# Second macaron step of a hybrid trunk layer: ten of 22 hidden tiles by seven block products

## The chip, the cores and the metric

The kernel runs on one core of a Trainium2 chip. The core has a matrix engine (TensorE, PE in the profile; its weight loads are shown apart as PEld), VectorE (DVE), ScalarE (ACT), GpSimd (POOL) and SyncE (SP), which issues the transfers. Each engine works through its own queue in order and waits on semaphores that the others raise. The metric is device time in microseconds, of the whole program, median of several runs.

## What is computed

One layer of a decoder trunk over 512 tokens of 1024 features, all in float32: a macaron half-step with a gated feed-forward, a mixer (attention and a state-space branch), a second macaron half-step, a gated embedding, a last norm. The change is in the second half-step, which is this, with `x` of 512 x 1024, `w1` and `w3` of 1024 x 2816 and `w2` of 2816 x 1024:

```python
def rmsnorm(x, g):
    y = xf * lax.rsqrt(jnp.mean(xf * xf, axis=-1, keepdims=True) + EPS)
    return (y * g.astype(jnp.float32)).astype(x.dtype)

def swiglu(x, w1, w3, w2):
    return (jax.nn.silu(x @ w1) * (x @ w3)) @ w2

h = h + 0.5 * swiglu(rmsnorm(h, g_ffn2[i]), w1_b[i], w3_b[i], w2_b[i])
```

`x @ w1` is called the gate product here, `x @ w3` the linear product. The 2816 hidden features are 22 tiles of 128.

## The kernel before

Activations lie transposed, features on the 128 partitions and the 512 tokens along the row, so the residual stream is eight tiles `X[k]` of 128x512. Matmuls take 128x128 of a weight as the stationary operand and 128x512 of the activation as the moving one. For accuracy each float32 operand is split into a rounded high part and the remainder, and each product is three matmuls (`mm3`, lines 234 to 237): high x high, low x high, high x low. The split of a weight half (128x512, four 128x128 blocks, loaded whole from HBM into `wraw`, five buffers) is a cast on ACT for the high part (`split_w`, L159) and a subtraction on DVE for the low part (helper `tt`, L74).

The work is a list of units, each with its weight sources, its steps of matmuls and the operations that follow a step. `run` goes through the units step by step and writes the instructions out in that order; nothing reorders them later. At the start of a step it casts the weights that the next unit will need (`convert`), then issues the evictions that have come due, then chains, then deferred work and the subtractions of the new weights, then the step's matmuls. An eviction listed as `(step, d, fn)` is issued `d` steps after the next step begins. So on ACT and DVE the place in the queue is set by these numbers alone.

A half-step (`ffn_units`) works in three parts of 7, 7 and 8 hidden tiles. For every hidden tile there is a unit for the gate product and one for the linear product, each two steps of 12 matmuls; then come eight output tiles of the down projection over the tiles of the part, `X[m] += 0.5 * ...`. The evictions of a tile: `gate_a` multiplies the gate product by the norm's row `nrm.r` on DVE and takes the tanh on ACT, `gate_b` forms silu up to a factor on DVE, `lin_a` scales the linear product on DVE, `lin_b` multiplies the two on DVE and casts the high part of the hidden tile on ACT (L369), `lin_c` subtracts for the low part on DVE. `lin_a` has d = 0 and `lin_b` has d = 1 (0 for the last tile of a part).

After this half-step comes the gate of the embedding (`gate_units`). Twelve of its sixteen weight halves are split ahead of time, two per unit, in units counted from the end of the half-step's list: `U2[j // 2 - 20]`. They go into four buffers of tag `m2` and into the shared pool `g4` of 27 buffers, where the normed inputs and the hidden tiles lie too.

Of the kernel before, what the change touches and what calls it, by code (L numbers as in the profile page):

```python
# [15 lines left out]
L = 512  # L16
# [5 lines left out]
EPS = 1e-6  # L22
FIRST = [(0, 2), (2, 4), (4, 8)]
PREP = 5
FEW = 3
SCORES = [(n, n + 1, n + 2) for n in (0, 4, 8, 12)]
VALUES = [7, 11, 15, 18]
# [14 lines left out]
def hybrid_trunk_kernel(ctx: ExitStack, tc: tile.TileContext, xT, pT, w13a, w2a, w13b, w2b, wqk, wv, ws, wf,  # L42
# [71 lines left out]
    selr = const.tile([128, 8], F32R, name="selr")  # L114


    qsel = [const.tile([128, L], F32R, name=f"qsel{j}") for j in range(2)]
    kcum = [const.tile([128, L], F32R, name=f"kcum{j}") for j in range(2)]
    HALF = [slice(0, 64), slice(64, 128)]


# [65 lines left out]
    def convert(u, nxt, h):  # L187

        last = h == len(u.steps) - 1
        res = []  # L190
        if nxt is not None:
            res = [(nxt, i) for i in range(len(nxt.srcs)) if nxt.parts[i] is None and (i == h or last)]
        return res + [(v, i) for hh, v, i in u.extra if hh == h]

    def order_weights(units):
# [8 lines left out]
    def run(units):  # L204
        while dma_at[0] < RAWS:
            wdma()
        for ui, u in enumerate(units):
            nxt = units[ui + 1] if ui + 1 < len(units) else None
            for f in u.starts:
                f()  # L210
            for h, step in enumerate(u.steps):
                rest = [split_w(v, i) for v, i in convert(u, nxt, h)] if u.ahead else []
                run_posts(evicts)
                advance(chains)
                while late:
# [23 lines left out]
    def gemm_steps(box, key, rhs, n, half=None):  # L239


        h = min(4, n)

        def part(k0, k1):
            def f(u):
                if k0 == 0:
                    box[key] = bank()
                for k in range(k0, k1):
                    mm3(box[key], *u.w(k if half is None else half * 4 + k % 4), *rhs(k), k == 0, k == n - 1)
            return f  # L250
        return [part(0, h), part(h, n)]
# [90 lines left out]

    PARTS = [range(0, 7), range(7, 14), range(14, 22)]

    def ffn_units(nrm, w13, w2, final, skip_first=False):
        units = []
        ready = lambda: nrm.r is not None
        for pi, part in enumerate(PARTS):
            hid = {}
            for f in part:  # L350
                box = {}

                def gate_a(box=box):
                    box["t"] = tmp(base="t1")
                    tt(box["t"], box[0], nrm.r, MUL)
                    box["h"] = tmp(base="th")
                    act(box["h"], box["t"], AF.Tanh, scale=0.5)

                def gate_b(box=box):
# [12 lines left out]
                def lin_c(box=box, hid=hid, f=f):  # L372
                    tt(hid[f][:, 1, :], box["t"], raw32(hid[f][:, 0, :]), SUB)

                if f == 0 and skip_first:
                    units.append((box, [(1, 0, gate_a), (1, 1, gate_b), (1, 1, lin_a), (1, 2, lin_b),
                                        (1, 3, lin_c)], ready))
                    continue
                e = 0 if f == part[-1] else 1
                after = [[(0, gate_a), (1, gate_b)], [(0, lin_a), (e, lin_b), (e + 1, lin_c)]]  # L380
                if f == 0:

                    steps = [[gemm_steps(box, wi, nrm.pair, KD, wi)[h] for wi in range(2)] for h in range(2)]
# [1224 lines left out]
```

## Time and profile before

| | us |
|---|---|
| median of three runs | 1006.03 (1005.78 to 1007.55) |
| profiled execution, device time | 1005.87 |
| its span, first to last instruction | 1004.1 |
| PE busy | 992.2 |
| DVE busy | 642.5 |
| ACT busy | 419.1 |
| POOL busy | 85.5 |

The second macaron step runs from about 594 to 950 us of the span. Matmuls are pipelined and the ends of their records are modelled, so a matmul's cost is read from the distance between the starts of neighbours, not from its duration. DVE and ACT records overlap a little for the same reason: what an operation costs its queue is the distance to the next start.

### The profile page before, as it was taken

To read this page: it belongs to the slowest core of one execution; us is meant where nothing else is said; L and a number is where in the kernel's file an instruction comes from. 1 tells how busy PE (TensorE), PEld (TensorE's weight loads), DVE (VectorE), ACT (ScalarE), POOL (GpSimd) and SP (SyncE) were. 2 spreads that over 40 slices of the span, in tenths; PEclk is the share of its full clock that TensorE was granted. 3 is DMA by queue.
4 is the path that set the end of the run, shared out by engine and by line. 5 is a ranking of instruction groups with operands and counts; after the bars stand their busy time and mean duration, and the time that the engine had idled before them with its cause. 6 is when DMAs were issued, how large, how long until landed. Compare 5 with 4: busy or idle time off the path is not lost.

```text
span 1004.1 us, 13382 instructions
## 1 busy us (share of the span) xinstructions
PE 992.2 (99%) x4800; PEld 826.5 (82%) x4800; DVE 642.5 (64%) x1252; ACT 419.1 (42%) x793; POOL 85.5 (9%) x87
## 2 busy tenths in 40 slices
PE   9999999999999999999999999999999999999996
PEld 7888888888878889887888888888888888888876
DVE  6668788767755555889987865443454436646443
ACT  6333233332244444469995443322333224434232
POOL 0440000001000001004651010000000000000000
PEclk9999999999999999999999999999999999999999
DMA  6432332323245332222212233333323334533101
GB/s 210 146 96 83 110 103 92 88 84 108 95 109 129 94 95 74 64 64 73 79 60 74 87 114 95 102 92 100 100 89 97 93 105 148 168 103 95 43 35 49
DMA packets 56915, 96.57 MB, mean 96 GB/s; under 512 B 10176, under 2 KB 14912, under 8 KB 56848
## 3 DMA queue, kind: packets, MB, share of 16 engines
q1 hardware_dynamic: 56432, 94.62, 30.8%
q0 software_dynamic: 416, 1.08, 0.3%
q8 instruction: 38, 0.62, 0.3%
q14 instruction: 29, 0.24, 0.1%
HBM read 92.41 MB, written 2.10 MB: 94 GB/s over the span
## 4 chain that ended last, share of the span: by engine, by line
PE 86%; issue 9%; ACT 2%; DVE 1%; POOL 1%; DMA 1%; SPq 0%; POOLq 0%; DVEq 0%; ACTq 0%
PE ps L235 27%; PE ps L237 27%; PE ps L236 27%; PE ps L1487 1%; PE ps L1098 1%; POOL lg L1090 1%; DMA x<-xT 1%; PE ps L315 0%; PE ps L329 0%; PE ps L1144 0%; PE ps L1143 0%; PE ps L647 0%; ACT gt L80 0%; ACT xhl L80 0%; SPq L1458 0%
## 5 line engine op out<-in xcount | busy, mean ns | idle before, releaser
L235 PE MATMUL ps<-xhl,whi 128*128 128x512 f32 x816 | 320.3, 393 | 0.0
L237 PE MATMUL ps<-xhl,whi 128*128 128x512 f32 x816 | 317.8, 389 | 0.0
L236 PE MATMUL ps<-xhl,wlo 128*128 128x512 f32 x816 | 317.7, 389 | 0.0
L159 ACT CAST whi<-wraw 128x512 fp32r<-128x512 f32 x324 | 195.9, 607 | 239.9 <-PE ps L237 177.0
L74 DVE TENSOR_TENSOR wlo<-wraw,whi 128x512 fp32r<-128x512 f32 x324 | 216.7, 674 | 5.8 <-ACT whi L159 5.6
L237 PEld LDWEIGHTS ps<-xhl,whi 128*128 128x128 f32 x816 | 153.2, 188 | 32.3
L235 PEld LDWEIGHTS ps<-xhl,whi 128*128 128x128 f32 x816 | 153.2, 188 | 31.9 <-issue 1.0
L236 PEld LDWEIGHTS ps<-xhl,wlo 128*128 128x128 f32 x816 | 153.3, 188 | 31.2
L235 PE MATMUL ps<-h,whi 128*128 128x512 f32 x352 | 137.3, 390 | 0.0
L237 PE MATMUL ps<-h,whi 128*128 128x512 f32 x352 | 137.0, 389 | 0.0
L236 PE MATMUL ps<-h,wlo 128*128 128x512 f32 x352 | 137.0, 389 | 0.0
L77 DVE SCALAR_TENSOR_TENSOR x<-ps,x 128x512 f32<-128x512 f32 x48 | 33.2, 691 | 95.2 <-PE ps L237 95.1
L77 DVE SCALAR_TENSOR_TENSOR t<-ps,rbc 128x512 f32<-128x512 f32 x44 | 30.3, 690 | 76.3 <-PE ps L237 76.3
L236 PEld LDWEIGHTS ps<-h,wlo 128*128 128x128 f32 x352 | 66.1, 188 | 13.7
L237 PEld LDWEIGHTS ps<-h,whi 128*128 128x128 f32 x352 | 66.1, 188 | 13.7
L235 PEld LDWEIGHTS ps<-h,whi 128*128 128x128 f32 x352 | 66.1, 188 | 13.7
L74 DVE TENSOR_TENSOR t<-ps,rbc 128x512 f32<-128x512 f32 x44 | 30.4, 691 | 71.1 <-PE ps L237 65.0
L80 ACT ACTIVATE th<-t 128x512 f32<-128x512 f32 x44 | 27.8, 632 | 91.1 <-DVE t L74 91.1
L369 ACT CAST h<-t 128x512 fp32r<-128x512 f32 x44 | 27.4, 622 | 81.3 <-DVE t L74 81.3
L319 POOL TENSOR_TENSOR rc<-ms,mhalf 128x4 f32<-128x4 f32 x6 | 8.1, 1344 | 519.2 <-DVE ms L318 519.2
L1090 POOL TENSOR_SCALAR lg<-lg,rs 128x128 f32<-128x128 f32 (+3 forms) x32 | 37.8, 1196 | 97.9 <-issue 78.7
L80 ACT ACTIVATE xhl<-x,colt 128x512 fp32r<-128x512 f32 x32 | 23.0, 725 | 47.9 <-DVE x L77 41.0
(254 smaller groups left out, 1104.0 us busy)
## 6 DMA issues: line engine op xcount, KB each, us to landing
wraw<-w13b SPq DMA_DIRECT2D x88, 256.0 KB, 2.9
wraw<-w13a SPq DMA_DIRECT2D x84, 256.0 KB, 2.8
wraw<-w2a SPq DMA_DIRECT2D x32, 256.0 KB, 2.7
wraw<-w2b SPq DMA_DIRECT2D x32, 256.0 KB, 2.7
wraw<-wqk SPq DMA_DIRECT2D x16, 256.0 KB, 2.8
wraw<-wout SPq DMA_DIRECT2D x16, 256.0 KB, 2.7
wraw<-wgate SPq DMA_DIRECT2D x16, 256.0 KB, 2.8
wraw<-w2a SPq DMA_DIRECT2D x16, 192.0 KB, 2.4
```

The lines of the kernel that those rows point to most:

```text
L74: V.tensor_tensor(out, a, b, op)
L77: V.scalar_tensor_tensor(out, a, s, b, op0, op1)
L80: S.activation(out, in_, f, **kw)
L159: S.copy(hi[:, 0:n], w[:, 0:n])
L235: T.matmul(ps, lh, rh, start=start, stop=False)
L236: T.matmul(ps, ll, rh, start=False, stop=False)
L237: T.matmul(ps, lh, rl, start=False, stop=stop)
L319: G.tensor_tensor(rc[:, 0:n], ms[:, 0:n], mhalf[:, 0:n], ALU.pow)
L369: S.copy(hl[:, 0, :], box["t"])
L1090: G.tensor_scalar(x, x, rs[h2][:, j:j + 1], None, MUL)
L1098: T.transpose(ps[:, j * 128:(j + 1) * 128], lg[h2][:, j * 128:(j + 1) * 128], ident)
L1487: T.matmul(box0[wi], fw[wi][2 if i == 1 else 1][:, k], n1.pair(k)[i == 2], start=k + i == 0, stop=k + i == KD + 1)
```

## The change

Twelve tiles stay as they were ("plain"), ten become "quick", by the string `PLAIN`: tiles 3, 5, 7, 9, 11, 13, 14, 16, 18 and 20. A quick tile takes its gate and linear products together as a product of 2x2 blocks: the weights in four blocks (gate and linear, first and second half of the 1024 features), the input in four (first and second half of the features, lower and upper 256 tokens). In place of eight block products it forms seven, from sums of blocks (Winograd's form of Strassen's scheme). Each of the seven is a step of 4 slices x 3 passes, 12 matmuls with 256 columns. They collect in two PSUM banks: several products add onto the same area, and between them ACT copies the area out (`p1`, `p5`, `u2`, `u3`).

The sums of weights are formed on POOL from four whole blocks, which are loaded into four spare tiles (`qsel` and `kcum` of the attention, now in a pool) with two more for results (`maskp` and a buffer of `rbc`). Each of the seven weight operands is split as before, cast on ACT and subtraction on DVE, into the four `m2` buffers, three steps ahead of its product (`AHEAD`). The differences of the input are formed once, during the first tiles (`halves`): scaled copies on ACT, differences on POOL, split on ACT and DVE, eight more tiles of `g4`. `beside` puts the sums and splits at steps of the units around the quick tile, by the nominal step lengths in `lasts`. Because `g4` is fuller now, the early splits of the gate weights move to the last eight units of the half-step (`U2[j // 2 - 8]`).

The core of the diff:

```diff
+PLAIN = 'PPPQPQPQPQPQPQQPQPQPQP'
...
-    qsel = [const.tile([128, L], F32R, name=f"qsel{j}") for j in range(2)]
-    kcum = [const.tile([128, L], F32R, name=f"kcum{j}") for j in range(2)]
+    qsel = [spare_tile(F32R, "qsel") for _ in range(2)]
+    kcum = [spare_tile(F32R, "kcum") for _ in range(2)]
...
+            self.hooks, self.lasts = {}, [2.72] * len(steps)
...
+                rest += [f for f in [f() for f in u.hooks.get(h, [])] if f]
                 run_posts(posts)
...
+    def halves(nrm, goff):
...
+        for k in range(4):
+            xa, xb, ta, tb = [tmp(base="xt") for _ in range(4)]
+            act(xa, X[k], AF.Copy, scale=colt[:, goff + k:goff + k + 1])
+            act(xb, X[k + 4], AF.Copy, scale=colt[:, goff + k + 4:goff + k + 5])
+            G.tensor_tensor(ta[:, 0:HT], xa[:, HT:], xa[:, 0:HT], SUB)
+            G.tensor_tensor(tb[:, 0:HT], xb[:, HT:], xa[:, HT:], SUB)
+            G.tensor_tensor(ta[:, HT:], xb[:, HT:], ta[:, 0:HT], SUB)
+            G.tensor_tensor(tb[:, HT:], xb[:, 0:HT], ta[:, HT:], SUB)
...
+            for t, dst in ((ta, nrm.ta), (tb, nrm.tb)):
+                hl = g4([128, 2, L], F32R, "xth")
+                S.copy(hl[:, 0, :], t)
+                dst[k] = hl
+                defer(1, lambda t=t, hl=hl: tt(hl[:, 1, :], t, raw32(hl[:, 0, :]), SUB))
+
+    def quick_unit(nrm, w13, f, hid, last, seq):
...
+        def take(i):
+            def g():
+                src = spare((A11, 4, 5, A12, A21, 5, A22)[i])
+                t = m2t([128, 2, 512], F32R, "wq")
+                hi, lo = t[:, 0], t[:, 1]
+                S.copy(hi, src)
+                ops[i] = hi, lo
+
+                def rest():
+                    tt(lo, src, raw32(hi), SUB)
+                    if i == 2:
+                        G.tensor_tensor(src, spare(A12), src, SUB)
+                    done = {0: A11, 3: A12, 4: A21, 6: A22}.get(i)
+                    if done is not None and seq.get(f):
+                        seq[f](done)
+                return rest
+            return g
...
+                out = box[0][:, 0:HT] if i in (0, 2, 4, 6) else box[1][:, HT:] if i in (1, 5) else box[1][:, 0:HT]
+                hi, lo = ops.pop(i)
+                for k in range(4):
+                    ks = slice(k * 128, k * 128 + 128)
+                    first = k == 0 and i < 2
+                    T.matmul(out, hi[:, ks], moving(i, k, 0), start=first, stop=False, skip_group_check=i > 1)
+                    T.matmul(out, lo[:, ks], moving(i, k, 0), start=False, stop=False, skip_group_check=i > 1)
+                    T.matmul(out, hi[:, ks], moving(i, k, 1), start=False, stop=k == 3, skip_group_check=i > 1)
...
+        def p1(box=box):
+            box["t"] = tmp(base="t1")
+            S.copy(box["t"][:, 0:HT], box[0][:, 0:HT])
...
+        def gate_a(box=box):
+            t = box["t"]
+            tt(t, box[1], t, ADD)
+            tt(t, t, nrm.r, MUL)
...
+        d = (0, 0, 0, 1, 1) if last else (0, 1, 1, 2, 3)
+        u = Unit([], [product(i) for i in range(KINDS)],
+                 [(0, 0, p1), (1, 0, p5), (2, 0, u2), (4, 0, u3), (5, 0, gate_a), (5, 0, lin_a)]
+                 + [(6, e, fn) for e, fn in zip(d, (gate_b, gate_c, lin_b, hid_a, hid_b))])
+        u.lasts = [1.45] * KINDS
+
+        plan = [(-7, add(4, A21, A22, ADD)), (-6, add(5, 4, A11, SUB)), (-5, add(A21, A11, A21, SUB))]
+        plan += [(i - AHEAD, take(i)) for i in range(KINDS)]
...
+                if plain is not None and plain[f] == "Q":
+                    units.append(quick_unit(nrm, w13, f, hid, f == part[-1], seq))
+                    continue
...
-    U2 = ffn_units(n3, w13b, w2b, lambda m: n4.add(m, X[m]))
+    U2 = ffn_units(n3, w13b, w2b, lambda m: n4.add(m, X[m]), plain=PLAIN)
...
+    chain_at(U2[0], halves(n3, G_FFN2))
...
-        U2[j // 2 - 20].extra.append((j % 2, u_g[j // 2], j % 2))
+        U2[j // 2 - 8].extra.append((j % 2, u_g[j // 2], j % 2))
```

Two places show what this does to the queues. The first is ACT at the end of tile 4's linear product and the start of tile 5. Before (`th` and `h` of L369 are tile 4's, the casts `whi` are weights of tiles 5 and 6, plain both):

```order
L80 ACTIVATE th_1290_6156<-t1_1289_6154 128x512
L159 CAST whi_1293_6174<-wraw_1273_6074 128x512
L159 CAST whi_1296_6193<-wraw_1277_6094 128x512
L159 CAST whi_1301_6214<-wraw_1281_6114 128x512
L369 CAST h_1303_6218<-t1_1289_6154 128x512
L159 CAST whi_1305_6235<-wraw_1286_6136 128x512
L80 ACTIVATE th_1308_6241<-t1_1307_6239 128x512
```

Now, with tile 5 quick (`wq` are its seven weight operands, L444, L448 and L451 the copies `p1`, `p5` and `u2` out of its PSUM areas):

```order
L81 ACTIVATE th_1316_6276<-t1_1315_6274 128x512
L406 CAST wq_1317_6278<-sum_1235_5852 128x512
L406 CAST wq_1318_6280<-maskp_99 128x512
L406 CAST wq_1320_6300<-sum_1237_5854 128x512
L406 CAST wq_1322_6318<-sum_1236_5853 128x512
L546 CAST h_1324_6336<-t1_1315_6274 128x512
L444 COPY t1_1325_6338<-ps_1323_6322 128x256
L406 CAST wq_1326_6340<-sum_1233_5850 128x512
L448 COPY t3_1328_6358<-ps_1327_6344 128x256
L406 CAST wq_1329_6360<-sum_1237_5854 128x512
L451 COPY t1_1325_6338<-ps_1323_6322 128x256
```

Four casts of the quick tile stand before the cast of tile 4's hidden tile (L546, the old L369), and the first copy out of tile 5's PSUM stands right behind that cast.

The second is DVE at the same boundary. Before, from `gate_a` of tile 4 on (`t3` is the scaled linear product, the row with two `t1` is the multiplication of `lin_b`):

```order
L74 TENSOR_TENSOR t1_1289_6154<-ps_1282_6116,rbc_1223_5849 128x512
L74 TENSOR_TENSOR wlo_1288_6151<-wraw_1268_6051,whi_1287_6150 128x512
L77 SCALAR_TENSOR_TENSOR t1_1289_6154<-th_1290_6156,t1_1289_6154 128x512
L74 TENSOR_TENSOR wlo_1294_6175<-wraw_1273_6074,whi_1293_6174 128x512
L77 SCALAR_TENSOR_TENSOR t3_1298_6196<-ps_1292_6161,rbc_1223_5849 128x512
L74 TENSOR_TENSOR wlo_1297_6194<-wraw_1277_6094,whi_1296_6193 128x512
L74 TENSOR_TENSOR t1_1289_6154<-t1_1289_6154,t3_1298_6196 128x512
L74 TENSOR_TENSOR wlo_1302_6215<-wraw_1281_6114,whi_1301_6214 128x512
L74 TENSOR_TENSOR h_1303_6218<-t1_1289_6154,h_1303_6218 128x512
```

Now (`h_1314` is the hidden tile of the quick tile 3, whose evictions reach into tile 4):

```order
L75 TENSOR_TENSOR t1_1315_6274<-ps_1310_6236,rbc_1242_5882 128x512
L75 TENSOR_TENSOR wq_1317_6278<-sum_1235_5852,wq_1317_6278 128x512
L75 TENSOR_TENSOR wq_1318_6280<-maskp_99,wq_1318_6280 128x512
L75 TENSOR_TENSOR h_1314_6272<-th_1308_6229,h_1314_6272 128x512
L78 SCALAR_TENSOR_TENSOR t1_1315_6274<-th_1316_6276,t1_1315_6274 128x512
L75 TENSOR_TENSOR wq_1320_6300<-sum_1237_5854,wq_1320_6300 128x512
L78 SCALAR_TENSOR_TENSOR t3_1321_6316<-ps_1319_6285,rbc_1242_5882 128x512
L75 TENSOR_TENSOR wq_1322_6318<-sum_1236_5853,wq_1322_6318 128x512
L75 TENSOR_TENSOR t1_1315_6274<-t1_1315_6274,t3_1321_6316 128x512
L75 TENSOR_TENSOR wq_1326_6340<-sum_1233_5850,wq_1326_6340 128x512
L75 TENSOR_TENSOR h_1324_6336<-t1_1315_6274,h_1324_6336 128x512
```

From the scaled linear product on, the three operations stand as before, with a weight subtraction of the quick tile where one of the next plain tile stood; ahead of them stand two operations more than before.

## Rows read from the trace of the kernel before

**Rows 1.** The page, part 1: busy us, share of the span, instructions.
```profile
PE 992.2 (99%) x4800; PEld 826.5 (82%) x4800; DVE 642.5 (64%) x1252; ACT 419.1 (42%) x793; POOL 85.5 (9%) x87
```

**Rows 2.** Waits of PE: who, released by whom: us in total, times, longest.
```profile
PE ps L108 <- POOL ones L96: 1.3, 1, 1.3
```

**Rows 3.** Windows: length, busy us of PE, PEld, DVE, ACT, POOL, PEclk, DMA, GB/s.
```profile
600.00:644.00 44.00, 44.00 (x196) 36.45 (x195) 25.12 (x40) 14.91 (x26) 0.00 (x0) 1.00 0.29 92
...
828.00:862.00 34.00, 34.00 (x152) 28.16 (x151) 23.22 (x38) 16.57 (x28) 0.00 (x0) 1.00 0.48 155
...
990.30:996.40 6.10, 6.10 (x52) 5.98 (x50) 2.23 (x4) 2.06 (x6) 1.29 (x1) 1.00 0.19 73
```

**Rows 4.** Timeline of PE: start us, us, instruction; one product's first matmul, the next's.
```profile
707.15 0.39 PE L235 MATMUL ps<-xhl,whi 128*128 128x512 f32 x1
...
712.59 0.39 PE L235 MATMUL ps<-xhl,whi 128*128 128x512 f32 x1
```

**Rows 5.** Timeline of PE, the last product of the kernel, 256 columns.
```profile
990.49 0.36 PE L235 MATMUL ps<-gw,xhl 128*128 128x256 f32 x1
990.69 0.28 PE L236 MATMUL ps<-gw,xhl 128*128 128x256 f32 x1
...
996.21 0.28 PE L237 MATMUL ps<-gw,xhl 128*128 128x256 f32 x1
```

**Rows 6.** Timeline of DVE: `gate_a` of a plain tile, then the boundary to the next.
```profile
707.35 0.69 DVE L74 TENSOR_TENSOR t<-ps,rbc 128x512 f32<-128x512 f32 x1 [3.54 <-PE ps L237]
...
712.79 0.69 DVE L77 SCALAR_TENSOR_TENSOR t<-ps,rbc 128x512 f32<-128x512 f32 x1 [2.75 <-PE ps L237]
713.40 0.68 DVE L74 TENSOR_TENSOR wlo<-wraw,whi 128x512 fp32r<-128x512 f32 x1
714.00 0.68 DVE L74 TENSOR_TENSOR t<-t,t 128x512 f32<-128x512 f32 x1
```

**Rows 7.** Timeline of ACT, same tile.
```profile
708.07 0.63 ACT L80 ACTIVATE th<-t 128x512 f32<-128x512 f32 x1 [2.82 <-DVE t L74]
708.61 0.60 ACT L159 CAST whi<-wraw 128x512 fp32r<-128x512 f32 x1
...
714.72 0.62 ACT L369 CAST h<-t 128x512 fp32r<-128x512 f32 x1 [1.26 <-DVE t L74]
```

**Rows 8.** Timeline of ACT and PE where PE waits for a cast.
```profile
956.06 1.65 ACT L159 CAST gw<-wraw 128x512 fp32r<-128x512 f32 x3
...
956.71 0.50 PE L235 MATMUL ps<-gw,xhl 128*128 128x512 f32 x1 [0.37 <-ACT gw L159]
...
957.05 0.39 PE L236 MATMUL ps<-gw,xhl 128*128 128x512 f32 x1
```

**Rows 9.** Lines, shapes apart: xcount, busy us, mean ns, idle before.
```profile
L159 ACT CAST whi<-wraw 128x512 fp32r<-128x512 f32 x292 | 179.5, 618 | 204.4 <-PE ps L237 147.5 <-ACT whi L159 28.6 <-issue 18.2
L842 ACT COPY gel<-ps 128x256 f32<-128x256 f32 x4 | 1.4, 358 | 0.0
L74 DVE TENSOR_TENSOR o<-gt,ps 128x256 f32<-128x256 f32 x2 | 0.8, 421 | 0.1
```

**Rows 10.** Lines of POOL, shapes apart.
```profile
L1090 POOL TENSOR_SCALAR lg<-lg,rs 128x512 f32<-128x512 f32 x8 | 12.9, 1625 | 0.0
L1090 POOL TENSOR_SCALAR lg<-lg,rs 128x256 f32<-128x256 f32 x8 | 7.9, 991 | 0.0
L1380 POOL TENSOR_TENSOR o<-o,gfb 128x512 f32<-128x512 f32 x1 | 1.3, 1294 | 5.3 <-ACT gt L80 5.3
```

**Rows 11.** Timeline of DVE and POOL in the attention.
```profile
468.12 1.46 POOL L1090 TENSOR_SCALAR lg<-lg,rs 128x256 f32<-128x256 f32 x1
...
468.72 0.96 DVE L74 TENSOR_TENSOR wlo<-wraw,whi 128x512 fp32r<-128x512 f32 x1
```

**Rows 12.** The tile qkhl: durations in ns, least, median, most; first and last start.
```profile
L74 DVE TENSOR_TENSOR qkhl<-qk,kcum x8: 674/838/1171, 454.6 to 504.2; 64x512 fp32r<-64x512 f32 x8
```

**Rows 13.** The loads of w13b, from issue to landing.
```profile
DMA to landing us min/median/max: 2.6/2.9/4.8
```

More of the change, by code (lines that the diff above doesn't have):

```diff
@@ L114, in hybrid_trunk_kernel, with spare_tile, spare @@
     selr = const.tile([128, 8], F32R, name="selr")
-    qsel = [const.tile([128, L], F32R, name=f"qsel{j}") for j in range(2)]
-    kcum = [const.tile([128, L], F32R, name=f"kcum{j}") for j in range(2)]
+    def spare_tile(dt, base):
+        return pool.tile([128, L], dt, name=nm(base), tag="spare", bufs=4)
+    qsel = [spare_tile(F32R, "qsel") for _ in range(2)]
+    kcum = [spare_tile(F32R, "kcum") for _ in range(2)]
+    spares = []
+    def spare(i):
+        if not spares:
+            spares.extend(spare_tile(F32, "sum") for _ in range(4))
+            spares.append(maskp)
+            spares.append(pool.tile([128, L], F32, name=nm("sum"), tag="rbc", bufs=2))
+        return spares[i]
     HALF = [slice(0, 64), slice(64, 128)]
@@ L191, in convert @@
         if nxt is not None:
-            res = [(nxt, i) for i in range(len(nxt.srcs)) if nxt.parts[i] is None and (i == h or last)]
+            res = [(nxt, i) for i in range(len(nxt.srcs)) if nxt.parts[i] is None and (i == h - (len(u.steps) - 2) or last)]
         return res + [(v, i) for hh, v, i in u.extra if hh == h]
@@ L343, in hybrid_trunk_kernel @@
     PARTS = [range(0, 7), range(7, 14), range(14, 22)]
-    def ffn_units(nrm, w13, w2, final, skip_first=False):
+    HT = L // 2
+    def halves(nrm, goff):
+        nrm.ta, nrm.tb = [None] * 4, [None] * 4
+        for _ in range(2):
+            yield
+        for k in range(4):
[6 more added lines that the diff above has]
+            G.tensor_tensor(tb[:, HT:], xb[:, 0:HT], ta[:, HT:], SUB)
+            for _ in range(4):
+                yield
+            for t, dst in ((ta, nrm.ta), (tb, nrm.tb)):
[3 more added lines that the diff above has]
+                defer(1, lambda t=t, hl=hl: tt(hl[:, 1, :], t, raw32(hl[:, 0, :]), SUB))
@@ new lines, in quick_unit, with load, add, g @@
+    def quick_unit(nrm, w13, f, hid, last, seq):
+        A21, A22, A11, A12 = range(4)
+        KINDS, AHEAD = 7, 3
+        srcs = [w13[f, wi][:, c * 512:(c + 1) * 512] for wi, c in ((1, 0), (1, 1), (0, 0), (0, 1))]
+        ops = {}
+        def load(i):
+            nc.sync.dma_start(spare(i), srcs[i])
+        def add(o, a, b, op):
+            def g():
+                G.tensor_tensor(spare(o), spare(a), spare(b), op)
+            return g
+        def take(i):
+            def g():
+                src = spare((A11, 4, 5, A12, A21, 5, A22)[i])
[11 more added lines that the diff above has]
+                return rest
+            return g
+        def moving(i, k, w):
+            lower, upper = slice(0, HT), slice(HT, L)
+            x, y = nrm.hl[k], nrm.hl[k + 4]
+            src, ts = ((x, lower), (nrm.ta[k], lower), (nrm.ta[k], upper), (y, lower), (nrm.tb[k], lower), (y, upper),
+                       (nrm.tb[k], upper))[i]
+            return src[:, w, ts]
+        box = {}
+        def product(i, box=box):
+            def g(u):
+                if i < 2:
+                    box[i] = bank()
+                out = box[0][:, 0:HT] if i in (0, 2, 4, 6) else box[1][:, HT:] if i in (1, 5) else box[1][:, 0:HT]
[6 more added lines that the diff above has]
+                    T.matmul(out, hi[:, ks], moving(i, k, 1), start=False, stop=k == 3, skip_group_check=i > 1)
+            return g
+        def p1(box=box):
+            box["t"] = tmp(base="t1")
+            S.copy(box["t"][:, 0:HT], box[0][:, 0:HT])
+        def p5(box=box):
+            box["u"] = tmp(base="t3")
+            S.copy(box["u"][:, 0:HT], box[1][:, HT:])
+        def u2(box=box):
+            S.copy(box["t"][:, HT:], box[0][:, 0:HT])
+        def u3(box=box):
+            S.copy(box["u"][:, HT:], box[0][:, 0:HT])
+        def gate_a(box=box):
+            t = box["t"]
+            tt(t, box[1], t, ADD)
+            tt(t, t, nrm.r, MUL)
+        def lin_a(box=box):
+            u = box["u"]
+            tt(u[:, HT:], u[:, HT:], u[:, 0:HT], ADD)
+        def gate_b(box=box):
+            box["h"] = tmp(base="th")
+            act(box["h"], box["t"], AF.Tanh, scale=0.5)
+        def gate_c(box=box):
+            stt(box["t"], box["h"], 1.0, box["t"], ADD, MUL)
+            tt(box["t"], box["t"], nrm.r, MUL)
+        def lin_b(box=box):
+            h, t = box["h"], box["t"]
+            stt(h[:, HT:], box["u"][:, HT:], 0.5, t[:, HT:], MUL, MUL)
+            stt(h[:, 0:HT], box[0][:, 0:HT], 0.5, t[:, 0:HT], MUL, MUL)
+        def hid_a(box=box, f=f):
+            hl = g4([128, 2, L], F32R, "h")
+            S.copy(hl[:, 0, :], box["h"])
+            hid[f] = hl
+        def hid_b(box=box, f=f):
+            tt(hid[f][:, 1, :], box["h"], raw32(hid[f][:, 0, :]), SUB)
+        d = (0, 0, 0, 1, 1) if last else (0, 1, 1, 2, 3)
[5 more added lines that the diff above has]
+        plan += [(i - AHEAD, take(i)) for i in range(KINDS)]
+        if not seq["units"]:
+            plan += [(-16, lambda i=i: load(i)) for i in range(4)]
+        else:
+            seq[seq["f"]] = load
+        seq["f"] = f
+        seq["units"].append((u, plan))
+        return u
@@ new lines, in beside @@
+    def beside(units, quick):
+        at, t = [], 0.0
+        where = {}
+        for u in units:
+            where[id(u)] = t
+            for h, n in enumerate(u.lasts):
+                at.append((t, u, h))
+                t += n
+        todo = []
+        for u, plan in quick:
+            todo += [(where[id(u)] + s_ * 1.45 + 0.01, fn) for s_, fn in plan]
+        for t, fn in sorted(todo, key=lambda p: p[0]):
+            _, u, h = [a for a in at if a[0] <= t][-1]
+            u.hooks.setdefault(h, []).append(fn)
@@ L346, in ffn_units @@
+    def ffn_units(nrm, w13, w2, final, skip_first=False, plain=None):
         units = []
+        seq = {"units": [], "f": None}
         ready = lambda: nrm.r is not None
@@ L418, in ffn_units @@
                 units.append(Unit(srcs, gemm_steps(box, 0, pair, n), [(1, 0, res(box, m))]))
+        if seq["units"]:
+            beside(units, seq["units"])
         return units
```

## The prediction

> **What bounds the kernel now.** I read the busy shares first: TensorE (PE) is busy 99% of the span, VectorE (DVE) 64% [rows 1]. Then the list of waits of PE: six entries, all small, the longest the one shown [rows 2]. Then the windows over the second macaron step (594 to 950 us), which say by stage that none of the six lies there: in 600 to 644 us PE is busy all 44.00 us while DVE has 25.1 and ScalarE (ACT) 14.9; in 828 to 862, where each 5.44 us carry four weight halves and not two, still no hole [rows 3]. So the time of this step is the number of matmuls times their distance, and anything else matters only where it makes PE wait. Last I read the distances. A 512-column matmul starts 226.7 ns after the one before: 707.15 to 712.59 us holds the 24 matmuls of one product, 5.44 us [rows 4]. A 256-column one, each with its own 128x128 weight load as here, starts every 120.0 ns: 46 steps from 990.69 to 996.21 us [rows 5]. Halving the columns does not quite halve the time, and the change has to live with that.
>
> **What TensorE gets.** A plain tile is two products of 8 slices and 3 passes, 48 matmuls of 512 columns: 48 x 226.7 ns = 10.88 us. A quick tile is seven products of 4 slices and 3 passes, 84 matmuls of 256 columns: 84 x 120.0 ns = 10.08 us. That is 0.80 us a tile, 8.0 us for ten, if no product starts late. One eighth of the arithmetic goes (one product of eight), but only 7.4% of the time.
>
> The Trainium skill ("TensorE: Matmul & The Clock Gate", Back-to-back issue gap) gives an isolated gap of columns / 2.4 + 2.5 ns; by it a plain tile takes 10.36 us, a quick one 9.17, and ten tiles would save 11.9 us. The rows are 11 ns above it at both widths, and the rows decide.
>
> **What the other engines get, and what hides it.** Per quick tile DVE has seven weight subtractions where a plain one has four, and in all 12 operations of 512 columns and 3 of 256: 12 x 0.60 us (the distance of neighbours in [rows 6]) + 3 x 0.42 [rows 9] = 8.5 us. A plain tile has nine, 5.4 us. A pair makes 13.9 of 20.96 us. ACT has nine operations of 512 and four copies of 256 columns, at 0.54 to 0.62 and 0.36 us [rows 7, 9]: about 7 us, in a pair about 11. GpSimd (POOL) has four sums; the one 128x512 two-input operation of the trace took 1.29 us, a one-input one beside a busy DVE 1.63 [rows 10], so 5.2 to 6.5 of 20.96 us, and its results are due some 3 us or more after it can finish. None of the three is full, so these are free unless they stand in a queue ahead of something that PE needs at once. The loads are the same bytes; each quick tile's four are issued during the quick tile before it, more than 10 us ahead, and land in 2.6 to 4.8 us [rows 13].
>
> The differences of the normed input (16 POOL operations of 256 columns at up to 0.99 us [rows 10], 16 ACT operations of some 0.6 to 0.7, 8 subtractions) fall in the first three plain tiles, 32.6 us, in which ACT is a third busy and POOL idle [rows 3]. Free; if this cover fails, a weight half of tile 0 or 1 comes late by a cast or two, about a microsecond, once.
>
> The twelve early weight halves of the gate stage move from the tiles into the last down-projection units. There a unit of 5.44 us has four subtractions, a residual addition, an input subtraction and a sum: 7 x 0.60 to 0.69 = 4.2 to 4.8 us on DVE. Window 828 to 862 shows four halves per unit at 155 GB/s without a hole [rows 3]; I cost it at nothing. If the cover goes, a cast and a subtraction late, 1.3 us, in up to six units: 8 us.
>
> **Where a product does start late.** The third product of a quick tile adds into the PSUM area of the first, so it must wait until ACT has copied the first out. In ACT's new order that copy (L444) stands behind the cast of the plain tile before (L546), and this cast waits for two steps on DVE with a weight subtraction between them. The plain kernel has the same three DVE operations at the same place, so the trace times them. Count from the end of the plain tile's matmuls, 712.59 us in the trace [rows 4]: DVE starts the linear product's scaling at +0.20, the weight subtraction at +0.81, the multiplication at +1.41, ending +2.09 [rows 6]; ACT's cast starts at +2.13 [rows 7]. ACT's next operation starts up to 0.09 before the end of this one (the pair at 708: 708.07 + 0.63 against 708.61 [rows 7]), so at +2.66, and a copy of 256 columns takes 0.36 [rows 9]: +3.02. PE is on its way 0.05 after a cast [rows 8], +3.07. The third product is due after 24 matmuls, at 24 x 0.120 = +2.88. Late by 0.19. The first matmul after a break has its weight load uncovered: 0.20 to the next instead of 0.12 [rows 5], and 0.34 instead of 0.227 [rows 8]; so 0.08 to 0.11 more. Together 0.27 us. After that ACT's copies and casts run 0.7 us or more ahead of PE, so it happens once a tile.
>
> It happens in the eight quick tiles that follow a plain one; 7 and 14 follow a down-projection, with no such cast in front. 8 x 0.27 = 2.2 us.
>
> One thing is added that the plain trace does not have at this place: the fourth sum on POOL (L412) is released by DVE's subtraction just before, and so runs under the three operations of this chain. POOL beside DVE costs DVE sometimes nothing and sometimes much: a subtraction that met a POOL operation took 0.96 us [rows 11] and not 0.68 [rows 6], and the worst of its kind 1.17 [rows 12]. Bounds for the chain: nothing, or 0.49 for each of three operations, 1.5. Most operations met by POOL in the trace were not slowed, so I take 0.1 us. A tile then loses 0.37, eight lose 3.0.
>
> Sum: -8.0 + 3.0 = -5.0 us on the profiled 1005.87 us (span 1004.1 and 1.8 around it), so 1000.9; on the median of the runs, 0.16 higher, **1001.0 us**.
>
> **Rivals.**
> *No wait.* ACT or DVE runs ahead of this count by 0.2 us and the copy is in time: 1006.0 - 8.0 = 998.0. For it: the miss is small beside 2.88. Against: the chain begins with the end of the plain tile's matmuls, which nothing can move. 0.15.
>
> *DVE one operation late.* The plain tile's `gate_a` starts 5.44 - 0.20 = 5.24 us before its end; the tanh follows 0.72 later, the quick tile's first cast 0.54 after that and ends 0.62 on [rows 6, 7], at -3.36. Then DVE has five operations in front of the chain, to -0.36 by 0.60 each, and the chain is released at +0.20: 0.56 to spare. If that is used up, the chain starts an operation later, and each of eight tiles loses 0.37 + 0.60 = 0.97 us: 7.8, which leaves 1005.8, no change. For it: the same line of DVE now holds three more weight subtractions. Against: 0.56 us is almost a whole operation. 0.12. Partial cases between this and the forecast (a gain of 2 to 3 us) 0.05.
>
> *POOL stands in DVE's way.* If every two-input operation of DVE beside POOL takes the worst 1.17 [rows 12] where its neighbours stand 0.60 apart, the multiplication ends at +0.20 + 3 x 1.17 = +3.71 instead of +2.09, a tile loses 0.27 + 1.62 = 1.9 us, eight lose 15.1, and the kernel takes 1013. It decides from a loss of 1.0 us a tile, 8.0 / 8. For it: two-input sums on POOL are heavier than the one-input operations of the trace. Against: one sum covers at most two of the three operations, and one of these reads PSUM. 0.08.
> The Trainium skill ("GPSIMD Engine Reference", Key points) has the rule of this rival: POOL shares its SBUF interfaces with VectorE, with contention for DVE instructions with two SBUF inputs. The 0.96 us of [rows 11] agrees; that most such meetings cost nothing does not.
>
> **How the numbers follow.** Forecast, a loss of 0.1 to 0.6 us in eight tiles, so a gain of 3 to 7 us: 0.60. With the rivals above that makes 1.00. A measurement of this kernel tells about 0.2% (2 us) from no change. Faster by more: forecast, no wait and the partial cases, 0.80; same: one operation late, 0.12; slower: POOL, 0.08. The range goes from a little under the case without a wait, 997.8, to the near edge of the case of no change, 1005.0; left out are the POOL case and half of that one, about 0.15 with what lies below.
>
> **What the new profile would show.** Right: matmuls of the quick lines 120 ns apart inside a product; a hole on PE of 0.2 to 0.5 us before the third product, in eight tiles and not in 7 and 14, its releaser ACT's copy (t1, L444); no other wait of PE from 600 to 950 us; the granted clock at 1.00, as over the 48 narrow matmuls now [rows 3]. Wrong: distances over 125 ns inside a product (840 such matmuls, so each ns takes 0.84 us off the 8.0); PE released by DVE's subtractions in several products of a tile (DVE is late as a whole); POOL sums over 2 us with DVE operations of 1 us beside them; holes in the last eight units of the step (the moved gate weights).

## The result, and the profile after

The changed kernel takes 1022.34 us (median of 4 runs, 1021.33 to 1023.6), the kernel before beside it 1005.94 (1005.78 to 1007.55): a ratio of 1.0159, 95% interval [1.0147, 1.0171]. It is 16.4 us slower. The forecast was 1001.0 us, 4.9 faster; the range ended at 1005.0.

The page, part 1, against [rows 1]: TensorE has 360 more matmuls and is busy 1.6 us less, in a span that is 16.4 us longer (1020.5 against 1004.1); GpSimd's busy time has nearly doubled.

```profile
PE 990.6 (97%) x5160; PEld 838.4 (82%) x5160; DVE 716.7 (70%) x1320; ACT 449.9 (44%) x879; POOL 160.5 (16%) x143
```

The waits of PE, where [rows 2] had nothing in this step. Three lines are new; the first is the place that the prediction names, the second it does not name.

```profile
PE ps L437 <- ACT t L444: 9.4, 8, 2.2
PE ps L252 <- DVE wlo L75: 7.5, 9, 1.3
...
PE ps L438 <- DVE wq L75: 1.0, 1, 1.0
```

The windows of [rows 3], and two short ones inside the first. PE, busy throughout before, is 4.2 and 1.9 us short. Behind the first breaks (PE busy 3.35 of 6.60 us) the granted clock is 0.55 for 3.80 us, the lower level of 1.2 GHz, and 19 matmuls take 3.80 us, not 19 x 0.120 = 2.28.

```profile
600.00:644.00 44.00, 39.79 (x206) 34.21 (x205) 37.22 (x44) 20.20 (x39) 19.26 (x15) 0.96 0.23 73
828.00:862.00 34.00, 32.13 (x220) 29.51 (x219) 23.67 (x33) 14.10 (x29) 6.79 (x5) 1.00 0.29 94
...
619.90:626.50 6.60, 3.35 (x26) 2.83 (x24) 5.66 (x8) 1.62 (x5) 1.48 (x2) 1.00 0.20 58
626.50:630.30 3.80, 3.77 (x19) 3.77 (x20) 2.01 (x4) 2.33 (x6) 0.00 (x0) 0.55 0.34 112
```

Two of the waits, in PE's timeline (start us, us, instruction). In quick tile 11 the third product starts 0.84 us after the matmul before it, not 0.12, and the next comes 0.22 later. In plain tile 6 the first matmul that takes a low weight half comes after 1.41 us, not 0.227, the next after 0.34.

```profile
660.90 0.39 PE L253 MATMUL ps<-xhl,whi 128*128 128x512 f32 x1
661.13 0.39 PE L251 MATMUL ps<-xhl,whi 128*128 128x512 f32 x1
662.54 0.50 PE L252 MATMUL ps<-xhl,wlo 128*128 128x512 f32 x1 [1.02 <-DVE wlo L75]
662.88 0.39 PE L253 MATMUL ps<-xhl,whi 128*128 128x512 f32 x1
...
757.29 0.28 PE L438 MATMUL ps<-xth,wq 128*128 128x256 f32 x1
757.41 0.29 PE L439 MATMUL ps<-xth,wq 128*128 128x256 f32 x1
758.25 0.39 PE L437 MATMUL ps<-xth,wq 128*128 128x256 f32 x1 [0.56 <-ACT t L444]
758.47 0.28 PE L438 MATMUL ps<-xth,wq 128*128 128x256 f32 x1
```

So I add up, from 590 us on, by how much the distances between PE's matmuls exceed 226.7 and 120.0 ns (where that is over 0.05 us): 1.8 us before, 26.0 after.

| where | lost, us |
|---|---|
| before the third product: tile 3 2.41; tiles 5, 9, 11, 13 0.71 to 0.72; 16, 18, 20 1.81; 7 and 14 none | 10.7 |
| before the first low weight half: tiles 4, 6, 8, 10, 12 and the down-projection behind tile 13 1.09 to 1.50; tiles 15, 17, 19 0.39 to 0.42 | 8.9 |
| inside the first product of tile 3 | 1.2 |
| the clock at 0.55 | 1.5 |
| the instruction behind each of 18 breaks, 0.10 to 0.11 | 1.9 |

Together 24.2; with the 8.0 that the matmuls save this is +16.2, against +16.4 between the spans.

What makes DVE late stands in its timeline at the end of quick tile 5. Its operations with two SBUF inputs take 1.49, 1.52 and 1.77 us, against 0.68 for 512 columns in [rows 6] and 0.42 for 256 in [rows 9]; the one ahead of them, with a PSUM input, takes 0.69 as in [rows 6].

```profile
657.13 0.69 DVE L75 TENSOR_TENSOR t<-ps,t 128x512 f32<-128x512 f32 x1 [2.10 <-PE ps L439]
657.86 1.49 DVE L75 TENSOR_TENSOR t<-t,rbc 128x512 f32<-128x512 f32 x1
659.27 1.52 DVE L75 TENSOR_TENSOR t<-t 128x256 f32<-128x256 f32 x1
660.72 1.77 DVE L75 TENSOR_TENSOR wlo<-wraw,whi 128x512 fp32r<-128x512 f32 x1
```

Beside it run the three sums of the next quick tile, on POOL:

```profile
657.51 1.29 POOL L398 TENSOR_TENSOR maskp<-sum,sum 128x512 f32<-128x512 f32 x1 [8.57 <-DMA sum<-w13b]
658.88 1.63 POOL L398 TENSOR_TENSOR sum<-maskp,sum 128x512 f32<-128x512 f32 x1
660.46 1.47 POOL L398 TENSOR_TENSOR sum<-sum,sum 128x512 f32<-128x512 f32 x1
```

Read the ends. POOL's first ends at 658.80 and DVE's multiplication at 659.35, 0.55 later; POOL's second at 660.51, 1.16 after that; DVE's 256-column sum at 660.79, 0.28 later; POOL's third at 661.93, 1.14 later; the weight subtraction at 662.49, 0.56 later. Each ends about as long after the other engine's operation as it takes alone: they take turns. So it is in the whole trace: of DVE's operations with two SBUF inputs, all 29 of 512 columns that overlap one of the four sums and end after it end 0.55 us after it, and all nine of 256 columns 0.28 or 0.29. From 657.86 to 662.49, 4.6 us, DVE does what elsewhere takes 0.60 + 0.34 + 0.60 = 1.5 us: it is some 3 us late when the plain tile needs that weight half.

### The profile page after: what moved, and what is told of

The parts are those of the page before. It is cut to its first block, busy times and chain, and to the rows that moved or that the text cites. A ratio compares the mean times of both kernels' runs of the same rounds, so it can differ in the third digit from the quotient of the medians.

```text
span 1020.5 us, 14325 instructions
## 1 busy us (share of the span) xinstructions
PE 990.6 (97%) x5160; PEld 838.4 (82%) x5160; DVE 716.7 (70%) x1320; ACT 449.9 (44%) x879; POOL 160.5 (16%) x143
## 4 chain that ended last, share of the span: by engine, by line
PE 75%; issue 12%; DVE 9%; ACT 2%; DMA 1%; POOL 0%; SPq 0%; POOLq 0%; DVEq 0%; ACTq 0%
PE ps L252 21%; PE ps L251 21%; PE ps L253 21%; DVE t L75 3%; DVE wlo L75 3%; PE ps L437 2%; PE ps L439 2%; PE ps L438 2%; DVE wq L75 1%; PE ps L1667 1%; DVE t L78 1%; PE ps L1277 1%; DVE xth L75 1%; PE ps L331 0%; PE ps L345 0%
## 5 line engine op out<-in xcount | busy, mean ns | idle before, releaser
L252 PE MATMUL ps<-xhl,wlo 128*128 128x512 f32 x656 | 256.5, 391 | 6.3 <-DVE wlo L75 6.3
L251 PE MATMUL ps<-xhl,whi 128*128 128x512 f32 x656 | 258.3, 394 | 0.0
L253 PE MATMUL ps<-xhl,whi 128*128 128x512 f32 x656 | 255.6, 390 | 0.0
L174 ACT CAST whi<-wraw 128x512 fp32r<-128x512 f32 (+1 forms) x284 | 169.8, 605 | 160.6 <-PE ps L253 117.1
L75 DVE TENSOR_TENSOR wlo<-wraw,whi 128x512 fp32r<-128x512 f32 (+1 forms) x284 | 204.9, 728 | 5.6 <-ACT whi L174 5.5
L252 PEld LDWEIGHTS ps<-xhl,wlo 128*128 128x128 f32 x656 | 123.2, 188 | 33.9 <-DVE wlo L75 9.7
L253 PEld LDWEIGHTS ps<-xhl,whi 128*128 128x128 f32 x656 | 123.1, 188 | 25.8
L251 PEld LDWEIGHTS ps<-xhl,whi 128*128 128x128 f32 x656 | 123.2, 188 | 25.7 <-issue 1.0
L75 DVE TENSOR_TENSOR wq<-sum,wq 128x512 fp32r<-128x512 f32 x60 | 46.2, 771 | 28.5 <-ACT wq L406 28.5
L546 ACT CAST h<-t 128x512 fp32r<-128x512 f32 x34 | 21.1, 621 | 90.9 <-DVE t L75 90.9
L437 PE MATMUL ps<-xth,wq 128*128 128x256 f32 x160 | 46.3, 289 | 9.4 <-ACT t L444 9.4
L439 PE MATMUL ps<-xth,wq 128*128 128x256 f32 x160 | 45.9, 287 | 0.0
L438 PE MATMUL ps<-xth,wq 128*128 128x256 f32 x160 | 45.8, 286 | 0.0
```

The costliest lines, as they stand in the source:

```text
L75: V.tensor_tensor(out, a, b, op)
L174: S.copy(hi[:, 0:n], w[:, 0:n])
L251: T.matmul(ps, lh, rh, start=start, stop=False)
L252: T.matmul(ps, ll, rh, start=False, stop=False)
L253: T.matmul(ps, lh, rl, start=False, stop=stop)
L437: T.matmul(out, hi[:, ks], moving(i, k, 0), start=first, stop=False, skip_group_check=i > 1)
```

## The experiments

Times are medians; single runs stand beside the kernel before on the same chip (1005.8 to 1006.7). "Over" is the sum of excess distances as above (1.8 before, 26.0 after). A dropped or added line shifts the line numbers in a kernel's rows.

**Which sums cost it.** First all four sums are left out.

```
-        plan = [(-7, add(4, A21, A22, ADD)), (-6, ...), (-5, ...)]
+        plan = []
-            src = spare((A11, 4, 5, A12, A21, 5, A22)[i])
+            src = spare((A11, A22, A12, A12, A21, A22, A22)[i])
-                    if i == 2:
-                        G.tensor_tensor(src, spare(A12), src, SUB)
```

> The changed kernel with all four sums on GpSimd left out: the quick products take loaded blocks in their place, so the gate and linear products are not the reference's; casts, subtractions, matmuls and loads stay as many. Theory A (a two-input sum on GpSimd and a VectorE operation with two SBUF inputs run one after the other, and VectorE so comes late): the waits of about 11.5 us before the third product shrink to 0.2 to 0.3 us in eight tiles, those of about 9.9 us on a low weight half go; 997.9 + 2.2 + up to 2 for the first quick tile = 1000 to 1002 us. Rival B (VectorE's queue is simply too long with three more weight subtractions a tile, whatever GpSimd does): 1015 us or more.

1001.44 us against 1006.67: 5.2 less. Over 4.3: seven times 0.19 before a third product, 0.41 in tile 3, no wait on a low half. One wait of 0.2 us or more is left in this step (L435 and L442 are L437 and L444 here):

```profile
PE ps L435 <- ACT t L442: 0.2, 1, 0.2
```

All but the sums is thus about as forecast: -8.0, and a stall of 0.19 a tile with 0.10 more behind it (forecast 0.19 and 0.08). Rival B falls.

Only the fourth sum left out:

```
-                    if i == 2:
-                        G.tensor_tensor(src, spare(A12), src, SUB)
```

> The changed kernel with only the fourth sum (L412) left out: the sixth product takes the third sum's operand, so the result is not the reference's. Theory A with L412 as the cause of the late third product: those waits fall from 11.5 to about 2.2 us, the others stay: 1013 us. Theory A with the three sums as the cause of both: nothing moves, 1020 to 1022. Rival B: 1020 to 1022 as well, since VectorE's queue is as long.

1016.58 us. I missed by 3.6: the low halves wait as before (6.9 us on PE), and the third product still loses 1.04 to 1.09 us in tiles 5, 11, 16 and 18. The three sums put DVE back so far that in these tiles the chain behind the plain tile starts 0.9 us late.

Only the three sums left out:

```
-        plan = [(-7, add(4, A21, A22, ADD)), (-6, ...), (-5, ...)]
+        plan = []
-                        G.tensor_tensor(src, spare(A12), src, SUB)
+                        G.tensor_tensor(spare(5), spare(A12), spare(A22), SUB)
```

> The changed kernel with the three sums of L398 left out and the fourth kept (the quick products take loaded blocks where these sums stood, so the result is not the reference's). Theory A: the waits of plain tiles on a low weight half (9.9 us) go; the late third product stays where the fourth sum causes it: 1012 us; if the three sums make the third product late in part 3 too (1.8 us a tile and not 0.7), 1008. Rival B: 1020 to 1022.

1002.74 us, better than expected, because the edit does more than it says: its fourth sum no longer reads what a subtraction writes, so it ran at 653.46 us, where the three had stood, and the chain was free. One sum at that place costs nothing except in tile 3 (1.50 us there, against 0.41); this run says nothing on L412. So I left L412 where it is, and took the other three out (but for one, once, ahead of tile 3):

```
-        plan = [(-7, add(4, A21, A22, ADD)), (-6, ...), (-5, ...)]
+        plan = [] if seq["units"] else [(-7, add(5, A22, A11, SUB))]
-            src = spare((A11, 4, 5, A12, A21, 5, A22)[i])
+            src = spare((A11, A22, 5, A12, A21, 5, A22)[i])
```

> The changed kernel without the three sums of L398, the fourth (L412) at its own place in each tile, released by the subtraction before it (the operands are loaded blocks and what the fourth sum leaves, so the result is not the reference's). If the fourth sum alone holds up one operation of the chain by some 0.55 us (1.22 us and not 0.68), the third product is late by 0.72 us and not 0.19 in the tiles after a plain one: 1001.4 + 1.3 (first quick tile) + 7 x 0.53 = 1006.4 us. Rival (the chain is late only because the three sums have put VectorE back): 1001.5 to 1003 us.

1005.34 us, 3.9 above no sum. Seven third products lose 0.42 to 0.43 us, where 0.72 was expected, and tile 3 2.24. In tile 3 the one sum of L398 that is left runs at 616.50 us and holds up DVE too, so its loss does not belong to the fourth sum alone. The chain on DVE, and POOL's sum beside it:

```profile
725.73 0.69 DVE L78 SCALAR_TENSOR_TENSOR t<-ps,rbc 128x512 f32<-128x512 f32 x1 [0.45 <-PE ps L253]
726.33 0.93 DVE L75 TENSOR_TENSOR wq<-sum,wq 128x512 fp32r<-128x512 f32 x1
727.18 0.68 DVE L75 TENSOR_TENSOR t<-t,t 128x512 f32<-128x512 f32 x1
```

```profile
725.41 1.30 POOL L412 TENSOR_TENSOR sum<-sum,sum 128x512 f32<-128x512 f32 x1 [21.55 <-DVE wq L75]
```

POOL ends at 726.71, the subtraction at 727.26, 0.55 later. DVE stood idle ahead of the chain, so the sum began before it and held it up by 0.25 us. In the changed kernel DVE comes later, and the same subtraction takes 1.22 (tile 11) or 1.40 us (tile 16). In tile 16 the chain is late besides: PE begins the tile at 849.85, and the scaling ahead of the subtraction starts 1.11 us behind that, not 0.20.

```profile
850.96 0.68 DVE L78 SCALAR_TENSOR_TENSOR t<-ps,rbc 128x512 f32<-128x512 f32 x1
851.57 1.40 DVE L75 TENSOR_TENSOR wq<-sum,wq 128x512 fp32r<-128x512 f32 x1
```

That makes the 1.81 of tiles 16, 18 and 20: 0.19 as without sums, 0.91 from the late chain, 0.72 from the fourth sum.

By these single runs the fourth sum alone costs 3.9 us (1.7 in seven tiles, most of the rest in tile 3), the three alone 15.1, all four 20.9; some 2 us come from their meeting. The step by itself, from its norm's sum to the first matmul of the gate stage, says 3.7, 16.0 and 22.2: PE came to it at 593.6 to 595.2 us in these runs, which blurs the whole times.

**Two inputs or any work on POOL.**

```
-                G.tensor_tensor(spare(o), spare(a), spare(b), op)
+                G.tensor_scalar(spare(o), spare(a), half[:, 0:1], None, MUL)
-                        G.tensor_tensor(src, spare(A12), src, SUB)
+                        G.tensor_scalar(src, spare(A12), half[:, 0:1], None, MUL)
```

> The changed kernel with each sum on GpSimd replaced by a scaling of its first operand by one number, of the same 128x512 shape at the same place (the values are then not the reference's). Theory A in its narrow form (only two-input GpSimd operations hold VectorE up): like without sums, 1000 to 1003 us, with GpSimd still busy some 50 us more than without them. Theory A in its wide form (any GpSimd operation does): 1015 to 1022. Rival B: 1015 or more.

1002.66 us; the four POOL operations take 68.8 us in all, more than the sums' 58.8 in the changed kernel, and seven third products lose 0.19 (tile 3's 1.49). So POOL's busy time is not what costs. At the chain, DVE and then POOL:

```profile
644.01 0.69 DVE L78 SCALAR_TENSOR_TENSOR t<-ps,rbc 128x512 f32<-128x512 f32 x1 [0.45 <-PE ps L253]
644.61 0.68 DVE L75 TENSOR_TENSOR wq<-sum,wq 128x512 fp32r<-128x512 f32 x1
645.21 0.69 DVE L75 TENSOR_TENSOR t<-t,t 128x512 f32<-128x512 f32 x1
```

```profile
643.65 1.57 POOL L412 TENSOR_SCALAR sum<-sum,half 128x512 f32<-128x512 f32 x1 [8.87 <-DVE wq L75]
```

The subtraction starts 0.96 us behind the scaling, lies beside it for 0.61 us and takes 0.68; with the fourth sum alone it started 0.92 behind the sum and waited for its end. But a scaling holds VectorE up as well, earlier in its own time. The third one of a tile, DVE and then POOL:

```profile
654.21 0.42 DVE L75 TENSOR_TENSOR t<-t 128x256 f32<-128x256 f32 x1
654.54 1.10 DVE L75 TENSOR_TENSOR wlo<-wraw,whi 128x512 fp32r<-128x512 f32 x1
```

```profile
654.13 1.85 POOL L398 TENSOR_SCALAR sum<-sum,half 128x512 f32<-128x512 f32 x1
```

DVE's first ends 1.35 us ahead of the scaling's end, its second 0.34 ahead, 0.42 late, and the scaling takes 1.85 and not 1.57. Under all 40 scalings the operations with two SBUF inputs end at least 1.35 us ahead of the scaling's end or at most 0.34 ahead of it. With 0.55 us for the operation that waited, a scaling shuts VectorE out for some 0.46 us, against some 1.15 of a sum (an estimate from these ends). So the engines take turns with one input too, but POOL's turn is less than half as long, and none fell where PE waits. The first scaling needs one block only and so starts a load earlier than the sum did, so part of the gain may be its place; for L412 the place is the same.

**The sums on VectorE**, at the same places of the program:

```
-                G.tensor_tensor(spare(o), spare(a), spare(b), op)
+                V.tensor_tensor(spare(o), spare(a), spare(b), op)
-                        G.tensor_tensor(src, spare(A12), src, SUB)
+                        V.tensor_tensor(src, spare(A12), src, SUB)
```

> The changed kernel with the four sums of each quick tile on VectorE and not on GpSimd, at the same places of the program; the result is the reference's. Theory A: 4 x 0.60 = 2.4 us more of VectorE a quick tile, but none of its operations held up: the three sums take 1.8 us of the some 1.9 us that the low weight half of the next plain tile has to spare, the fourth 0.6 of the 0.56 that the chain before the third product has: 1001 to 1004 us. Rival (VectorE full: what the sums cost there is what they cost now): 1010 or more.

1009.9 us: 12.4 less than the changed kernel, and still 4 above before; I missed by 6. The low halves wait once, for 0.7 us, but the third product loses 0.97 to 1.01 in each of seven tiles and 2.0 in tile 3. DVE's rows show why: `sum<-sum,sum`, and the line in front of it without a pause, so the chain starts late.

```profile
748.41 0.69 DVE L75 TENSOR_TENSOR wq<-sum,wq 128x512 fp32r<-128x512 f32 x1
749.13 0.69 DVE L412 TENSOR_TENSOR sum<-sum,sum 128x512 f32<-128x512 f32 x1
749.74 0.68 DVE L78 SCALAR_TENSOR_TENSOR t<-ps,rbc 128x512 f32<-128x512 f32 x1
750.35 0.68 DVE L75 TENSOR_TENSOR wq<-sum,wq 128x512 fp32r<-128x512 f32 x1
750.94 0.69 DVE L75 TENSOR_TENSOR t<-t,t 128x512 f32<-128x512 f32 x1
```

That is the prediction's rival of DVE one operation late, close to its price of 0.97 a tile; here it is the fourth sum that uses up the 0.56 us.

So the sums go later, the fourth out of the chain:

```
+        plan = [(-3.95, add(4, A21, A22, ADD)), (-3.9, add(5, 4, A11, SUB)), (-0.95, add(A21, A11, A21, SUB))]
+                    if i == 4:
+                        V.tensor_tensor(spare(5), spare(A12), spare(5), SUB)
+                        if seq.get(f):
+                            seq[f](A12)
+                    done = {2: A11, 4: A21, 6: A22}.get(i)
```

> Sums on VectorE, and later: the first two in the middle of the plain tile, the third in its last quarter, the fourth behind the fifth product's weight subtraction, out of the chain before the third product; the loads of two blocks are issued behind their last readers. The result is the reference's. Theory A: only the first quick tile (1.5 us) and 7 x 0.2 us before the third product are left: 997.9 + 2.9 = 1001 us, the time of the kernel without sums. Rival (VectorE full): 1005 or more.

1003.69 us. Seven third products lose 0.25 to 0.30, tile 3 2.3: the first part as expected, the first quick tile worse than the 1.5 I had put down.

Then the copy of the first product goes ahead of the h cast on ACT:

```
-                        evicts.append((slot_no[0] + d, f, u.need))
+                        evicts.insert(0 if d < 0 else len(evicts), (slot_no[0] + d, f, u.need))
-                 [(0, 0, p1), ...
+                 [(0, -1, p1), ...
```

> As the kernel with the sums on VectorE and later, and the copy of the first product (L444) put ahead of the plain tile's h cast on ScalarE. If the 0.19 us before the third product come from that cast, as the prediction has it, seven or eight of them go: 1.5 us less, 999.5 us. If they come from another wait they stay: 1001.

1001.79 us, 1.9 less. No third product is late any more; in tile 3 the fourth product is, by 1.40 us, and the fifth, by 0.51, which wait for later copies. So the cast in front was the prediction's 0.2 us.

**The first quick tile.** The 16 differences of the input on VectorE too:

```
-            G.tensor_tensor(ta[:, 0:HT], xa[:, HT:], xa[:, 0:HT], SUB)
+            V.tensor_tensor(ta[:, 0:HT], xa[:, HT:], xa[:, 0:HT], SUB)
...
```

> As the kernel before this one, and the 16 differences of the normed input (L373 to L376) on VectorE, 16 x 0.34 = 5.4 us in the first three plain tiles. If GpSimd's 256-column differences make the first quick tile late, its 1.3 us go: 998.2 us. If VectorE is too full in these tiles, a wait of 1 us or more appears there: 1000 or more.

1003.78 us: worse. DVE stands still at 604 us, with a weight subtraction queued behind the difference that waits for ACT:

```profile
603.15 0.69 DVE L75 TENSOR_TENSOR t<-t,t 128x512 f32<-128x512 f32 x1
606.20 0.42 DVE L373 TENSOR_TENSOR xt<-xt 128x256 f32<-128x256 f32 x1 [2.35 <-ACT xt L81]
...
607.96 0.69 DVE L75 TENSOR_TENSOR wlo<-wraw,whi 128x512 fp32r<-128x512 f32 x1
```

The differences one slot behind their inputs:

```
+            for _ in range(2):
+                yield
             V.tensor_tensor(ta[:, 0:HT], xa[:, HT:], xa[:, 0:HT], SUB)
...
-            for _ in range(4):
+            for _ in range(2):
                 yield
```

> As the kernel with everything on VectorE, but the differences of the normed input one slot of 2.72 us behind the ScalarE operations that they read, so that VectorE does not stand waiting for these. If that standing (some 2 us at 604 and 612 us) made the waits of 0.4 to 0.7 us in the first plain tiles and the late first quick tile, about 3 to 4 us go: 1000 us or less. If VectorE is simply too full there: 1002 or more.

999.54 us; 1.1 us is still lost in tile 3. The other way out is to leave the differences on GpSimd and start the quick tiles one later:

```
-PLAIN = 'PPPQPQPQPQPQPQQPQPQPQP'
+PLAIN = 'PPPPQPPQPQPQPQQPQPQPQP'
```

> The kernel with the sums on VectorE and the first product's copy ahead of the h cast, with the first quick tiles at 4 and 7 and not 3, 5 and 7: nine quick tiles, so 0.8 us of the gain go, and the 1.9 us lost in tile 3 behind GpSimd's differences should go too: 1000.7 us. If the first quick tile is late wherever it stands: 1002.6.

999.7 us with nine quick tiles; one step of PE in this half-step is over by more than 0.2 us. So in the first quick tile it is the neighbourhood that costs, not its being first.

**Ten quick tiles again** (the sums on DVE and later, the copy first, the first quick tile at 4; the differences on GpSimd):

```
-PLAIN = 'PPPQPQPQPQPQPQQPQPQPQP'
+PLAIN = 'PPPPQPQQPQPQPQQPQPQPQP'
```

> Ten quick tiles, the first at 4 (4, 6, 7, 9, 11, 13, 14, 16, 18, 20), the four sums on VectorE in the middle of the plain tile and behind the fifth product's subtraction, the first product's copy ahead of the h cast; the result is the reference's. Theory A: the matmuls' own saving of 8.0 us and no wait of TensorE left in the second half-step but tenths: 998 to 999.5 us, 0.993 of the kernel before. Rival (the last tile of the first part, now a quick one, starts the down-projection late): 1000 to 1002.

998.87 us (5 runs), against 1006.12: a ratio of 0.9926, interval [0.9912, 0.994]. Over is 1.8, as before: no stall is left. From the norm's sum to the gate stage the step takes 345.4 us and not 352.8: 7.4 of the 8.0 us arrive, and the rest lies in matmul distances of 227.1 and 120.2 ns in place of 226.7 and 120.0. The windows of [rows 3] again, DVE as busy as in the changed kernel (36.7 and 27.2 us against 37.2 and 23.7) and PE without a hole:

```profile
600.00:644.00 44.00, 44.00 (x235) 38.13 (x234) 36.72 (x53) 23.50 (x44) 9.66 (x10) 1.00 0.36 114
828.00:862.00 34.00, 34.00 (x219) 31.07 (x219) 27.17 (x45) 16.02 (x32) 0.00 (x0) 1.00 0.28 90
```

## Why the prediction was wrong

*TensorE, -8.0 us.* Right. Narrow matmuls stand 120 ns apart in the changed kernel too (757.29, 757.41), the wide ones 227; the kernel without a sum gains 5.2 us with its stalls, the last one 7.3 with none.

*The third product, 0.27 us in eight tiles.* Right in place, in cause, in size and in the tiles that are spared: 0.19 and 0.10 without a sum (0.41 in tile 3), gone when the cast stands behind the copy.

*The sum under the chain: "Most operations met by POOL in the trace were not slowed, so I take 0.1 us".* Too small: 0.24 with the fourth sum alone, 0.53 in tile 11, 0.72 in tile 16. "Most" counted the wrong operations. In the attention of the kernel before, 17 operations of 512 columns with two SBUF inputs meet one of the 32 scalings of L1090, and 9 of them take more than 0.70 us, up to 1.17; all 11 with a PSUM input take 0.67 to 0.69. The chain has two of the first kind, and [rows 10] has only one two-input operation of this size on POOL, from which its turn could not be read.

*"None of the three is full, so these are free unless they stand in a queue ahead of something that PE needs at once".* This step failed, and it holds about 15 of the 20.9 us. I asked when the sums' results are due, and not what runs on DVE while they run. They start when a load lands, which is when DVE has `gate_a`, `lin_a` and a weight subtraction to do at the end of a quick tile; these wait (4.6 us for 1.5 us of work at the end of tile 5), and the plain tile's low half comes late. Had I counted turns, DVE and POOL together would have had up to 13.9 + 5.2 to 6.5 of 20.96 us: little room on the whole, and none where DVE works without a pause.

*The POOL rival.* It had the mechanism, at 1013 and 0.08. It placed it under the fourth sum only, "one sum covers at most two of the three operations", and limited an operation to 1.17 us [rows 12]; with two inputs on POOL it is up to 1.77. The rule of the Trainium skill that stood beside it ("GPSIMD Engine Reference", Key points: contention for DVE instructions with two SBUF inputs) is borne out by these rows, and by the kernel before too: "that most such meetings cost nothing" was a misreading, as counted above.

*The differences of the input.* "Free; if this cover fails ... about a microsecond, once." The cover failed: 1.22 us instead of 0.68 for DVE operations beside them. Tile 3 is late by 0.4 us without sums; with them by 2.4 and 1.2, and 1.5 more go to the clock behind these breaks.

*The moved gate weights, the loads.* Right: the last eight units of the step show no new wait in the changed kernel.

*Signs named.* "POOL sums over 2 us" was not it: a sum reads 1.29 to 1.81 us. DVE's own rows show the turn, not POOL's.

## What to carry to other kernels

Before moving element-wise work to GpSimd, find what VectorE does in the same microseconds: a 128x512 sum there and an operation with two SBUF inputs on VectorE take turns, so it can cost more than the same operation put on VectorE, which took 0.60 us. Time the place, not the load: a step with slack on average can stand ahead of a chain with none. And check in the order of the queues that an experiment's edit has not freed an instruction to run elsewhere.

## What the runs showed of the hardware that was not expected

- GpSimd's 128x512 two-input operation and VectorE's operations with two SBUF inputs exclude each other: the later one ends its own time (0.55 us, POOL's 1.13 to 1.17) after the other's end. A VectorE operation with one PSUM input is not held (0.69).
- A one-input GpSimd operation of the same shape excludes them too, but only for some 0.46 us of its 1.57 (an estimate from the ends in the run with scalings): a subtraction that started 0.96 us behind it took 0.68, one that started 0.41 behind it 1.10.
- Behind the breaks of 1.2 us at 620 and 2.4 us at 624 the granted clock was 0.55 for 3.8 us; behind the single breaks of 1.8 us in tiles 16, 18 and 20 it stayed at 1.00.
